# A decoder trunk on one core: softplus behind the evacuation of k, v transposed into the shared score tile, entry weights scaled by ScalarE, the rest scaled in pieces

## The chip, the cores and the metric

The kernel runs on one core of one Trainium2 chip. The metric is the device time of one execution in microseconds. Each of the kernel's versions is timed in several runs, and the median counts.

## The reference

The program is a two-layer decoder trunk over 512 tokens of width 1024: a Mamba-2 layer, then a stick-breaking attention layer, each followed by a gated convolutional feed-forward block and a gated embedding. The change touches the attention and its way in. There, k and v come from one normalised projection, q from another with its own norm gain, and the attention of each of 16 heads is

```
z = einsum("bthd,bshd->bhts", q[:, q0:q1], k[:, :q1]) * scale
log_beta = log_sigmoid(z)
log_keep = where(causal, log_sigmoid(-z), 0.0)
log_rest = cumsum(log_keep, axis=3, reverse=True) - log_keep
w = where(causal, exp(log_beta + log_rest), 0.0)
out = einsum("bhts,bshd->bthd", w, v[:, :q1])
```

## The kernel before

All activations lie transposed: 128 features on the partitions, 512 tokens along the free axis. Every large product is done in three matmuls per 128x128 weight block, high part times low part, low times high, and high times high (L214 to L216), so that one product with 8 blocks is 24 matmuls of 128x512. Weights come from memory in units of 8 blocks, which one DMA loads (`raw`, L82, three buffers). Units of the q, k and v matrices are first multiplied by the norm's gain on GpSimd (L94, one instruction for a run of blocks). Then ScalarE rounds the unit into its high part (`whi`, L103) and VectorE takes the low part as a difference (`wlo`, L104). Units are made two ahead of their use.

The attention goes over 8 pairs of heads, p = 0 to 7. In steady state TensorE's order for one pair is written out by hand:

- the scores of pair p into five PSUM tiles (L754 to L775): one tile of two banks, of which only half of each bank is used (score part n = 0), and four of one bank (parts 1 to 4);
- `att_c(p-1, 0)`, weights times v for the first head of the pair before (L853), then the k product of pair p+1, then `att_c(p-1, 1)`;
- the q product of pair p+1, in whose middle v of pair p is transposed (`v_split`, L733) into an accumulator bank `pv`;
- `att_b(p)`, the suffix sums (L829), which add products of softplus(z) with a triangle of -1 onto the scores, in the order n = 1, 0, 2, 3, 4;
- the v product of pair p+1.

The products and `att_c` and `pv` share two accumulator banks. A product can start when the bank that was used two turns ago has been evacuated.

Between scores and suffix sums stands softplus, in `att_a`. ScalarE takes Abs and Exp of the five parts (L790, L791), loads another function table, and takes Ln (L794). For each part VectorE then adds max(z, 0) (`e`, L797) and rounds the high part (`sh`, L801), and GpSimd takes the low part (`sl`, L802). After the suffix sums ScalarE takes Exp (`w`, L832) and rounds (`wh`), and VectorE takes the low part (`wl`, L835). The other names: `t` is the evacuation of k or q out of the bank (L721) and `v` that of v (L726), `hi` and `lo` are the two parts of k, q or the output (L195, L196), `tp` and `e<-pav` evacuate `att_c` (L858, L859), `ot` is the low part of the output, and `vv` are the two parts of the transposed v (L738 on ScalarE, L739 on VectorE).

Only TensorE's order is by hand. On the other engines a scheduler sets the order when the program is built, from priorities, and each engine then works its queue strictly in that order. `tc.high_priority` moves instructions up, `tc.issue_after(x)` keeps them behind an instruction x.

On the way into the attention the last product of layer 0 (8 output tiles) feeds the residual, the squares for the norm (L230), their sum on GpSimd (`acc_sq`, L233) and on TensorE (`nsum`, L240), the reciprocal root on GpSimd (`ms`), eight small diagonal blocks on VectorE (`dg`), and their spread over the partitions (`nspr`, L275). Meanwhile q and k of pair 0 are multiplied into two further banks, `qa` and `ka`, then k of pair 1.

Of the kernel before, what the change touches and what calls it, by code (L numbers as in the profile page):

```python
# [67 lines left out]
class Weights:  # L68
# [3 lines left out]
    def __init__(self, nc, pool, src, ahead=2):  # L72
        self.nc, self.pool, self.src, self.ahead = nc, pool, src, ahead
        self.units, self.made, self.pos, self.gains = {}, 0, 0, {}

    def make(self, u, between=None):
        nc = self.nc
        raw = self.pool.tile([P, 8, P], F32, tag="raw", name="raw", bufs=3)
        cuts = 2 if u < 1 else 1
        parts = [slice(c * 8 // cuts, (c + 1) * 8 // cuts) for c in range(cuts)]  # L80
        for c, part in enumerate(parts):
            nc.sync.dma_start(  # L82
                out=raw[:, part].rearrange("p k m -> p (k m)"),
                in_=self.src[u][:, c * KD * P // cuts:(c + 1) * KD * P // cuts],
            )
            if between:
                between()
        i = 0
        while i < 8 and PLAN[8 * u][0] in self.gains:
            name, k, _ = PLAN[8 * u + i]  # L90
            n = 1
            while i + n < 8 and PLAN[8 * u + i + n][:2] == (name, k + n):
                n += 1
            nc.gpsimd.tensor_tensor(  # L94
                out=raw[:, i:i + n], in0=raw[:, i:i + n],
                in1=self.gains[name][:, k:k + n].unsqueeze(2).to_broadcast([P, n, P]), op=ALU.mult
            )
# [21 lines left out]
def tile_yoco(ctx: ExitStack, tc: tile.TileContext, xT, pT, prm, cst, csb, wdt, wts, out, dbg=None):  # L119
# [589 lines left out]
    ntri, nones, mask = cr[:, 0:128], cr[:, 128:256], cr[:, 256:512]  # L709
    identr = const.tile([P, P], F32R, name="identr")  # L710
    A.copy(out=identr, in_=ident)
    qs, ks, vs = {}, {}, {}

    def proj(name, m, hooks=None, bank=acc_bank):
        acc = bank()
# [2 lines left out]

    def qk_split(dst, p, acc, scale):
        t = S("t", 2)  # L720
        V.scalar_tensor_tensor(out=t, in0=acc, scalar=scale, in1=n_kv.r, op0=ALU.mult, op1=ALU.mult)  # L721
        dst[p] = split(t)

    def v_evac(p, acc):
        t = S("t", 2, name="v")
        V.tensor_tensor(out=t, in0=acc, in1=n_kv.r, op=ALU.mult)  # L726
        vs[p] = t

    def v_split(p):
        t = vs[p]  # L730
        pv = acc_bank("pv")
        for c in range(NCH):
            PE.transpose(out=pv[:, c * P:(c + 1) * P], in_=t[:, c * P:(c + 1) * P], identity=ident)  # L733
        pv4 = pv.rearrange("p (c i d) -> p c i d", c=NCH, i=2)
        vs[p] = []
        for i in range(2):
            vv = H(F32R, shape=(P, NCH, 2, 64), name="vv")
            A.copy(out=vv[:, :, 0], in_=pv4[:, :, i])  # L738
            V.tensor_tensor(out=vv[:, :, 1], in0=pv4[:, :, i], in1=vv[:, :, 0].bitcast(F32), op=ALU.subtract)  # L739
            vs[p].append(vv)  # L740
# [4 lines left out]

    def scores(p):

        two = two_banks("z")
        zs = [two[:, :, 0:256]] + [aux_bank("z") for _ in range(4)]
        ones_by = {}  # L750
        for n, parts in enumerate(PARTS):
            if n == 0:
                for i in range(2):
                    PE.matmul(two[:, i, 0:P], lhsT=identr, rhs=mask[:, 0:P], start=True, stop=False, skip_group_check=True)  # L754
                    ones_by[n, i] = two[:, i]
            elif n < 3:
                z = zs[n]
                PE.matmul(
                    z.rearrange("p (a b) -> p a b", b=P)[:, 0:2], lhsT=identr,
                    rhs=mask.rearrange("p (a b) -> p a b", b=P), start=True, stop=False, skip_group_check=True,  # L760
                )
            else:
                PE.matmul(zs[n][:, 0:P], lhsT=identr, rhs=mask[:, 0:P], start=True, stop=False, skip_group_check=True)
        todo = []
        for i in range(2):
            at = 0
            for n in TURNS[i]:
                own = [(b, c0 if n else 0) for h, b, c0 in PARTS[n] if h == i]
# [14 lines left out]

    def att_a(p):

        es, sp = {}, {}
        zs = scores(p)
        for n in (2, 0, 1, 3, 4):
            e = es[n] = S("d", 6, name="e") if n < 3 else S("c", 3, name="e")
            A.activation(out=like(n, e), in_=zs[n], func=AF.Abs)  # L790
            last = A.activation(out=e, in_=e, func=AF.Exp, scale=-1.0)  # L791
        with tc.issue_after(last.ins):
            for n in (2, 0, 1, 3, 4):
                ln = A.activation(out=es[n], in_=es[n], func=AF.Ln, bias=1.0)  # L794
        for n in (2, 0, 1, 3, 4):
            e = es[n]
            V.scalar_tensor_tensor(  # L797
                out=like(n, e), in0=zs[n], scalar=0.0, in1=like(n, e), op0=ALU.max, op1=ALU.add
            )
            hi, lo = H(F32R, name="sh"), H(F32R, name="sl")  # L800
            V.tensor_copy(out=hi, in_=e)  # L801
            G.tensor_tensor(out=lo, in0=e, in1=hi.bitcast(F32), op=ALU.subtract)  # L802
            sp[n] = (hi, lo)
        return zs, sp, ln

    def att_b(p, zs, sp, ln):

# [35 lines left out]
    def att_c(p, i, ws, bank=acc_bank):  # L843

        if i == 0:
            ots[p] = S("e", 3)
        ot = ots[p]
        po = bank("pav")
        mm = []
        for b, t_, f0 in ((0, ws[3 + i], 0), (1, ws[1 + i], 128), (2, ws[0], i * 256), (3, ws[1 + i], 0)):  # L850
            mm += [(po[:, b * P:], vs[p][i][:, b], s_[:, f0:f0 + T - b * P]) for s_ in t_]
        for n, (o_, l_, r_) in enumerate(mm):
            PE.matmul(  # L853
                o_, lhsT=l_.rearrange("p a d -> p (a d)"), rhs=r_, start=n == 0, stop=n == len(mm) - 1,
            )
        tp = S("th", 1, name="tp")
        with tc.high_priority(offset=300):
            A.copy(out=tp[0:64], in_=po[64:128])  # L858
            V.tensor_tensor(out=ot[LO[i]], in0=po[0:64], in1=tp[0:64], op=ALU.add)  # L859
        if i:  # L860
            if dbg:
                dbg("o", p, ot)
            o_t.append(split(ot, lo=S("ot", 8, F32R)))

    def qk(name, dst, p, scale, hooks=None):
        acc = proj(name, p, hooks)
        with tc.high_priority(offset=200):
            qk_split(dst, p, acc, scale)

    def v_proj(p):  # L870
        acc = proj("v", p)
        with tc.high_priority(offset=200):
            v_evac(p, acc)

    qa, ka = aux_bank("qa"), aux_bank("ka")
    product(qa, "q", 0, range(7), xg, stop=False)
    product(ka, "k", 0, range(7), xg, stop=False, hooks={5: n_kv.sums})
    product(qa, "q", 0, [7], xg, start=False)
    product(ka, "k", 0, [7], xg, start=False)
    qk("k", ks, 1, 1.0, hooks={3: n_kv.spread})  # L880
    with tc.high_priority(offset=400):
        qk_split(qs, 0, qa, 0.125)
        qk_split(ks, 0, ka, 1.0)
    ws = None
    for p in range(8):
        zz = att_a(p)
        if p:
            att_c(p - 1, 0, ws)
        if 0 < p < 7:
            qk("k", ks, p + 1, 1.0)  # L890
        elif p == 0:
# [115 lines left out]
```

## Time and profile before

| | |
|---|---|
| median of 3 runs | 1605.1 us (1603.92 to 1607.39) |
| the profiled execution | 1602.3 us, its span 1600.4 us |
| TensorE matmul busy | 1516.9 us (95%) |
| VectorE busy | 1023.1 us (64%) |
| ScalarE busy | 756.8 us (47%) |
| GpSimd busy | 345.1 us (22%) |
| mean granted TensorE clock | 0.971 |

The span runs from the first to the last instruction. Times in rows are microseconds from its start. Busy shares are averages over the whole program. The attention takes the stretch from about 840 to 1150 us, and there the mean granted clock of 50 us windows lies between 0.90 and 0.97.

### The profile page before, as it was taken

To read this page: it belongs to the slowest core of one execution; us is meant where nothing else is said; L and a number is where in the kernel's file an instruction comes from. 1 tells how busy PE (TensorE), PEld (TensorE's weight loads), DVE (VectorE), ACT (ScalarE), POOL (GpSimd) and SP (SyncE) were. 2 spreads that over 40 slices of the span, in tenths; PEclk is the share of its full clock that TensorE was granted. 3 is DMA by queue.
4 is the path that set the end of the run, shared out by engine and by line. 5 is a ranking of instruction groups with operands and counts; after the bars stand their busy time and mean duration, and the time that the engine had idled before them with its cause. 6 is when DMAs were issued, how large, how long until landed. Compare 5 with 4: busy or idle time off the path is not lost.

```text
span 1600.4 us, 18433 instructions
## 1 busy us (share of the span) xinstructions
PE 1516.9 (95%) x7082; PEld 1243.4 (78%) x7082; DVE 1023.1 (64%) x1334; ACT 756.8 (47%) x1152; POOL 345.1 (22%) x243
## 2 busy tenths in 40 slices
PE   7889999999999999999997999887999999999996
PEld 5677777788888888888886777776788888888885
DVE  6887888765567766622475876675567766652444
ACT  4365565644344443422444677766444444342343
POOL 3012424431110110101143533331211011010112
PEclk9999999999999999999998999999999999999998
DMA  5233332423333332333331111111233333333321
GB/s 175 78 112 121 97 126 86 125 80 92 94 104 93 93 105 93 111 100 93 93 91 53 53 53 53 40 41 45 72 97 96 95 101 95 96 108 93 94 90 53
DMA packets 44055, 143.67 MB, mean 90 GB/s; under 512 B 4896, under 2 KB 5152, under 8 KB 43968
## 3 DMA queue, kind: packets, MB, share of 16 engines
q1 hardware_dynamic: 43968, 142.51, 28.9%
q8 instruction: 55, 0.90, 0.2%
q14 instruction: 32, 0.26, 0.1%
HBM read 140.32 MB, written 2.16 MB: 89 GB/s over the span
## 4 chain that ended last, share of the span: by engine, by line
PE 75%; DVE 10%; ACT 8%; issue 3%; POOL 3%; DMA 1%; POOLq 0%; SPq 0%; ACTq 0%; DVEq 0%
PE acc L214 23%; PE acc L216 22%; PE acc L215 22%; PE z L829 3%; DVE wlo L104 2%; DVE c L328 2%; ACT d L494 1%; ACT whi L103 1%; DVE sh L801 1%; POOL y L522 1%; DVE e L797 1%; ACT e L790 1%; PE z L775 1%; ACT e L791 1%; DVE t L683 1%
## 5 line engine op out<-in xcount | busy, mean ns | idle before, releaser
L214 PE MATMUL acc<-hi,wlo 128*128 128x512 f32 x1776 | 714.6, 402 | 32.9 <-DVE t L721 19.8
L215 PE MATMUL acc<-lo,whi 128*128 128x512 f32 x1808 | 711.0, 393 | 0.0
L216 PE MATMUL acc<-hi,whi 128*128 128x512 f32 x1776 | 700.8, 395 | 0.0
L104 DVE TENSOR_TENSOR wlo<-raw,whi 128x1024 fp32r<-128x1024 f32 (+1 forms) x240 | 308.0, 1283 | 200.2 <-ACT whi L103 197.5
L214 PEld LDWEIGHTS acc<-hi,wlo 128*128 128x128 f32 x1776 | 339.6, 191 | 107.6 <-DVE t L721 20.7
L103 ACT CAST whi<-raw 128x1024 fp32r<-128x1024 f32 (+1 forms) x241 | 252.1, 1046 | 340.7 <-PE acc L216 285.2
L215 PEld LDWEIGHTS acc<-lo,whi 128*128 128x128 f32 x1808 | 344.5, 191 | 72.5 <-issue 3.4
L216 PEld LDWEIGHTS acc<-hi,whi 128*128 128x128 f32 x1776 | 338.9, 191 | 72.8
L328 DVE SCALAR_TENSOR_TENSOR c<-t,pm,c 128x511 f32<-128x511 f32 (+2 forms) x248 | 188.5, 762 | 5.8 <-ACT c L323 2.0
L233 POOL TENSOR_TENSOR acc_sq<-acc_sq,sq 128x512 f32<-128x512 f32 x60 | 87.1, 1452 | 400.8 <-ACT sq L230 350.6
L634 POOL TENSOR_TENSOR hf<-th,c 128x512 f32<-128x512 f32 x44 | 59.3, 1347 | 427.6 <-DVE c L328 388.2
L323 ACT ACTIVATE c<-t,pm 128x512 f32<-128x512 f32 x112 | 91.1, 814 | 14.1 <-DVE t L321 13.8
L321 DVE TENSOR_TENSOR t<-acc,r 128x512 f32<-128x512 f32 x112 | 76.7, 686 | 30.2 <-PE acc L216 26.7
L802 POOL TENSOR_TENSOR sl<-e,sh 128x512 fp32r<-128x512 f32 x40 | 57.5, 1439 | 86.3 <-DVE sh L801 83.1
L195 ACT CAST hi<-hf 128x512 fp32r<-128x512 f32 x44 | 26.8, 618 | 95.0 <-POOL hf L634 95.0
L94 POOL TENSOR_TENSOR raw<-raw,pm 128x1024 f32<-128x1024 f32 (+3 forms) x27 | 52.5, 1949 | 82.4 <-DMA raw<-in_wts 73.0
L196 DVE TENSOR_TENSOR lo<-hf,hi 128x512 fp32r<-128x512 f32 x44 | 32.3, 738 | 59.3 <-ACT hi L195 59.3
L631 ACT ACTIVATE th<-c 128x512 f32<-128x512 f32 x44 | 27.8, 632 | 80.8 <-DVE c L328 80.8
L494 ACT ACTIVATE d<-d,tok 128x128 f32<-128x128 f32 x128 | 44.7, 392 | 13.3 <-DMA d<-rows 12.8
L498 POOL TENSOR_TENSOR d<-d,cb 128x512 f32<-128x512 f32 x16 | 25.3, 1586 | 117.7 <-ACT btok L445 69.1
L632 DVE SCALAR_TENSOR_TENSOR th<-th,c 128x512 f32<-128x512 f32 x44 | 30.4, 691 | 30.6 <-ACT th L631 30.6
L230 ACT ACTIVATE sq<-x_k 128x512 f32<-128x512 f32 (+1 forms) x50 | 30.5, 615 | 34.5 <-DVE x_k L282 20.8
(193 smaller groups left out, 1522.6 us busy)
## 6 DMA issues: line engine op xcount, KB each, us to landing
raw<-in_wts SPq DMA_DIRECT2D x239, 512.0 KB, 3.6
d<-rows SPq DMA_DIRECT2D x32, 256.0 KB, 3.7
x_k<-in_xT SPq DMA_DIRECT2D x16, 256.0 KB, 4.9
out<-xo SPq DMA_DIRECT2D x8, 256.0 KB, 2.8
p_k<-in_pT SPq DMA_DIRECT2D x4, 256.0 KB, 3.0
raw<-in_wts SPq DMA_DIRECT2D x2, 256.0 KB, 4.1
pm<-in_prm SPq DMA_DIRECT2D x1, 312.0 KB, 6.4
cbt<-in_csb SPq DMA_DIRECT2D x1, 256.0 KB, 4.7
```

The source lines that it names most:

```text
L103: nc.scalar.copy(out=hi[:, part], in_=raw[:, part])
L104: e.tensor_tensor(out=lo[:, part], in0=raw[:, part], in1=hi[:, part].bitcast(F32), op=ALU.subtract)
L214: PE.matmul(acc, lhsT=wl, rhs=xh, start=start and n == 0, stop=False)
L215: PE.matmul(acc, lhsT=wh, rhs=xl, start=False, stop=False)
L216: PE.matmul(acc, lhsT=wh, rhs=xh, start=False, stop=stop and n == len(ks) - 1)
L233: G.tensor_tensor(out=self.acc, in0=self.acc, in1=t, op=ALU.add)
L321: V.tensor_tensor(out=t, in0=acc, in1=r, op=ALU.mult)
L323: A.activation(out=c, in_=t, func=AF.Identity, scale=w[:, f * taps + taps - 1:f * taps + taps], bias=b[:, f:f + 1])
L328: V.scalar_tensor_tensor(out=c[:, s:], in0=t[:, :T - s], scalar=w[:, i:i + 1], in1=c[:, s:], op0=ALU.mult, op1=ALU.add)
L494: A.activation(out=d[:, cs], in_=d[:, cs], func=AF.Relu, scale=-1.0, bias=acs[:, c * 32 + h:c * 32 + h + 1])
L634: G.tensor_tensor(out=hf, in0=th, in1=c1, op=ALU.mult)
L802: G.tensor_tensor(out=lo, in0=e, in1=hi.bitcast(F32), op=ALU.subtract)
```

## The change

Four edits are made together.

- Softplus is cut out of `att_a` into a function of its own that is called after `att_c(p-1, 1)`. Its VectorE instructions are kept behind the evacuation of the k product (of the v product for p = 0, of `att_c(6, 0)` for p = 7).
- v is transposed into the unused halves of the two-bank score tile (part 0). The bank `pv` is gone. The ScalarE and VectorE instructions that read the transposed v (`vv`) get a high priority.
- The weight units up to the second one from the start of k of pair 1 (four units) are scaled by ScalarE, in eight instructions of 128x128 each. The later units (twenty) stay on GpSimd, in pieces of 128x256, four for a unit.
- q and k of pair 0 are evacuated and split inside the product for k of pair 1, ahead of that product's own evacuation.

```diff
+        self.act_until = PLAN.index(("k", 0, 1)) // 8 + 2
...
+            if u < self.act_until:
+                for j in range(i, i + n):
+                    nc.scalar.activation(
+                        out=raw[:, j], in_=raw[:, j], func=AF.Identity, scale=self.gains[name][:, k + j - i:k + j - i + 1]
+                    )
+            else:
+                for j in range(i, i + n, 2):
+                    e = min(j + 2, i + n)
+                    nc.gpsimd.tensor_tensor(
+                        out=raw[:, j:e], in0=raw[:, j:e],
+                        in1=self.gains[name][:, k + j - i:k + e - i].unsqueeze(2).to_broadcast([P, e - j, P]),
+                        op=ALU.mult,
+                    )
...
     def v_split(p):
         t = vs[p]
-        pv = acc_bank("pv")
+        pv = twos.pop(p)[:, :, 256:512]
         for c in range(NCH):
-            PE.transpose(out=pv[:, c * P:(c + 1) * P], in_=t[:, c * P:(c + 1) * P], identity=ident)
+            PE.matmul(
+                pv[:, c // 2, c % 2 * P:(c % 2 + 1) * P], lhsT=t[:, c * P:(c + 1) * P], rhs=ident,
+                is_transpose=True, start=False, stop=False, skip_group_check=True,
+            )
...
+        with tc.high_priority(offset=300):
+            for i in range(2):
+                vv = H(F32R, shape=(P, NCH, 2, 64), name="vv")
+                v5 = vv.rearrange("p (a c) h d -> p a c h d", a=2)
+                src = pv4[:, :, :, i]
+                A.copy(out=v5[:, :, :, 0], in_=src)
+                V.tensor_tensor(out=v5[:, :, :, 1], in0=src, in1=v5[:, :, :, 0].bitcast(F32), op=ALU.subtract)
+                vs[p].append(vv)
...
-        two = two_banks("z")
+        two = twos[p] = two_banks("z")
...
+        return zs, es, ln
+
+    def softplus(zs, es):
+        sp = {}
         for n in (2, 0, 1, 3, 4):
...
-    qk("k", ks, 1, 1.0, hooks={3: n_kv.spread})
-    with tc.high_priority(offset=400):
-        qk_split(qs, 0, qa, 0.125)
-        qk_split(ks, 0, ka, 1.0)
+    def first():
+        n_kv.spread()
+        with tc.high_priority(offset=400):
+            qk_split(qs, 0, qa, 0.125)
+            qk_split(ks, 0, ka, 1.0)
+
+    qk("k", ks, 1, 1.0, hooks={3: first})
...
-        zz = att_a(p)
+        zs, es, ln = att_a(p)
         if p:
-            att_c(p - 1, 0, ws)
+            evac = att_c(p - 1, 0, ws)
         if 0 < p < 7:
-            qk("k", ks, p + 1, 1.0)
+            evac = qk("k", ks, p + 1, 1.0)
         elif p == 0:
-            v_proj(0)
+            evac = v_proj(0)
         if p:
             att_c(p - 1, 1, ws)
+        with tc.issue_after(evac.ins):
+            sp = softplus(zs, es)
```

The order on VectorE in pair 3, from the evacuation of `att_c(2, 0)` on. Before:

```order
L859 TENSOR_TENSOR e<-pav,tp 64x512
L797 SCALAR_TENSOR_TENSOR e<-z,e 128x512 x2
L801 CAST sh<-e 128x512
L797 SCALAR_TENSOR_TENSOR e<-z,e 128x512
L801 CAST sh<-e 128x512
L797 SCALAR_TENSOR_TENSOR e<-z,e 128x512
L721 SCALAR_TENSOR_TENSOR t<-acc,r 128x512
```

Now:

```order
L880 TENSOR_TENSOR e<-pav,tp 64x512
L731 SCALAR_TENSOR_TENSOR t<-acc,r 128x512
L818 SCALAR_TENSOR_TENSOR e<-z,e 128x512 x2
L206 TENSOR_TENSOR lo<-t,hi 128x512
L880 TENSOR_TENSOR e<-pav,tp 64x512
L818 SCALAR_TENSOR_TENSOR e<-z,e 128x512
L822 CAST sh<-e 128x512
L206 TENSOR_TENSOR ot<-e,hi 128x512
```

The evacuation `t` of k moved ahead of all of softplus. The low part of k, the evacuation of `att_c(2, 1)` and `ot` moved in between, ahead of the first or second `sh`.

The same queue up to `vv` in the same pair (the second `t` is the evacuation of q). Before:

```order
L801 CAST sh<-e 128x512
L859 TENSOR_TENSOR e<-pav,tp 64x512
L801 CAST sh<-e 128x512
L104 TENSOR_TENSOR wlo<-raw,whi 128x1024
L196 TENSOR_TENSOR lo<-t,hi 128x512
L196 TENSOR_TENSOR ot<-e,hi 128x512
L739 TENSOR_TENSOR vv<-pv,vv 128x4x64 x2
L721 SCALAR_TENSOR_TENSOR t<-acc,r 128x512
L104 TENSOR_TENSOR wlo<-raw,whi 128x1024
```

Now:

```order
L822 CAST sh<-e 128x512
L818 SCALAR_TENSOR_TENSOR e<-z,e 128x512
L822 CAST sh<-e 128x512
L818 SCALAR_TENSOR_TENSOR e<-z,e 128x512
L822 CAST sh<-e 128x512
L114 TENSOR_TENSOR wlo<-raw,whi 128x1024
L731 SCALAR_TENSOR_TENSOR t<-acc,r 128x512
L822 CAST sh<-e 128x512
L114 TENSOR_TENSOR wlo<-raw,whi 128x1024
L756 TENSOR_TENSOR vv<-z,vv 128x4x64 x2
```

The evacuation of q and the second `wlo` moved from behind `vv` to ahead of it.

The order on ScalarE in the same pair, from the last Ln on. Before:

```order
L794 ACTIVATE e<-e 128x512 x5
L103 CAST whi<-raw 128x1024
L858 COPY tp<-pav 64x512
L195 CAST hi<-t 128x512
L195 CAST hi<-e 128x512
L738 CAST vv<-pv 128x4x64 x2
L103 CAST whi<-raw 128x1024
L195 CAST hi<-t 128x512
L832 ACT_TABLE_LOAD
L832 ACTIVATE w<-z 128x512
```

Now:

```order
L811 ACTIVATE e<-e 128x512 x5
L113 CAST whi<-raw 128x1024
L205 CAST hi<-t 128x512
L879 COPY tp<-pav 64x512
L205 CAST hi<-e 128x512
L113 CAST whi<-raw 128x1024
L853 ACT_TABLE_LOAD
L853 ACTIVATE w<-z 128x512
L755 CAST vv<-z 128x4x64 x2
```

The two `vv` copies moved behind the first `w`, the Exp of part 1, which waits for the suffix sums of part 1 on TensorE.

On TensorE the order is the same in both. One wait on it is new in each pair: the first suffix sum of part 0 (L850 now, L829 before) waits for the second `vv` on VectorE, since both use the two-bank tile. On GpSimd each pair has its five `sl`, then the scaling of three units, in both; in three instructions before, in twelve now. On the way in, the sum of the last squares now stands behind the four pieces of one unit, and the reciprocal root behind those of a second.

## Rows read from the trace of the kernel before

**Rows 1.** TensorE's waits between 840 and 1240 us: total, times, longest.

```profile
PE acc L214 <- DVE t L721: 19.8, 6, 3.3
PE acc L214 <- DVE vv L739: 5.4, 1, 5.4
PE z L763 <- DVE t L721: 4.6, 2, 3.6
PE nsum L240 <- POOL acc_sq L233: 3.8, 1, 3.8
```

**Rows 2.** Stretches of pair 3: length, busy time by engine, granted clock, DMA.

```profile
973.55:979.54 5.99, 5.99 (x17) 4.72 (x17) 5.93 (x7) 1.21 (x2) 4.71 (x4) 0.50 0.00 0
979.54:993.18 13.64, 13.64 (x75) 11.84 (x73) 9.55 (x12) 9.29 (x15) 4.44 (x3) 1.00 0.26 78
```

**Rows 3.** The chain of waits: start, length; scores of pair 1, of pair 7.

```profile
894.47 2.11 PE z L775 x18
...
1093.28 1.07 PE z L775 x6
```

**Rows 4.** TensorE in pair 3 by time: start, length, line, tiles, shapes.

```profile
959.17 0.33 PE L754 MATMUL z<-cr,identr 128*128 128x128 f32 x2
...
968.63 0.39 PE L216 MATMUL acc<-hi,whi 128*128 128x512 f32 x1
...
982.41 0.39 PE L829 MATMUL z<-sh,cr 128*128 128x512 f32 x1
...
983.32 0.40 PE L829 MATMUL z<-sh,cr 128*128 128x256 f32 x2
...
987.66 0.45 PE L214 MATMUL acc<-hi,wlo 128*128 128x512 f32 x1
...
993.18 0.33 PE L754 MATMUL z<-cr,identr 128*128 128x128 f32 x2
```

**Rows 5.** VectorE in pair 3 by time.

```profile
968.95 1.29 DVE L797 SCALAR_TENSOR_TENSOR e<-z,e 128x512 f32<-128x512 f32 x2 [2.31 <-ACT e L794]
970.15 0.42 DVE L801 CAST sh<-e 128x512 fp32r<-128x512 f32 x1
...
971.09 1.21 DVE L801 CAST sh<-e 128x512 fp32r<-128x512 f32 x1
...
977.34 1.21 DVE L104 TENSOR_TENSOR wlo<-raw,whi 128x1024 fp32r<-128x1024 f32 x1
978.48 1.76 DVE L196 TENSOR_TENSOR lo<-t,hi 128x512 fp32r<-128x512 f32 x1
...
981.61 0.42 DVE L739 TENSOR_TENSOR vv<-pv,vv 128x256 fp32r<-128x256 f32 x1 [0.44 <-ACT vv L738]
```

**Rows 6.** GpSimd in pair 3 by time.

```profile
970.74 1.27 POOL L802 TENSOR_TENSOR sl<-e,sh 128x512 fp32r<-128x512 f32 x1 [3.30 <-DVE sh L801]
...
977.57 2.12 POOL L802 TENSOR_TENSOR sl<-e,sh 128x512 fp32r<-128x512 f32 x1 [0.43 <-DVE sh L801]
```

**Rows 7.** ScalarE in pair 3 by time.

```profile
968.28 2.71 ACT L794 ACTIVATE e<-e 128x512 f32<-128x512 f32 x5
970.90 1.03 ACT L103 CAST whi<-raw 128x1024 fp32r<-128x1024 f32 x1
...
981.21 0.37 ACT L738 CAST vv<-pv 128x256 fp32r<-128x256 f32 x1 [0.99 <-DVE vv L739]
...
985.53 0.60 ACT L832 ACTIVATE w<-z 128x512 f32<-128x512 f32 x1
```

**Rows 8.** All scalings of L94: ns shortest/median/longest, first and last start, shapes.

```profile
L94 POOL TENSOR_TENSOR raw<-raw,pm x27: 843/1899/2894, 814.1 to 1033.3; 128x1024 f32<-128x1024 f32 x22, 128x128 f32<-128x128 f32 x3, 128x896 f32<-128x896 f32 x1, 128x768 f32<-128x768 f32 x1
```

**Rows 9.** ScalarE's 128x128 activations elsewhere: busy us, mean ns.

```profile
L494 ACT ACTIVATE d<-d,tok 128x128 f32<-128x128 f32 x128 | 44.7, 392 | 13.3 <-DMA d<-rows 12.8
```

**Rows 10.** VectorE in pair 7: the first two `e`.

```profile
1102.73 1.29 DVE L797 SCALAR_TENSOR_TENSOR e<-z,e 128x512 f32<-128x512 f32 x2 [1.26 <-ACT e L794]
```

**Rows 11.** TensorE in pair 7: the first suffix sum.

```profile
1118.61 0.39 PE L829 MATMUL z<-sh,cr 128*128 128x512 f32 x1
```

More of the change, by code (lines that the diff above doesn't have):

```diff
@@ L93, in make @@
                 n += 1
[L94 to L97, printed above, removed]
+            if u < self.act_until:
[11 more added lines that the diff above has]
+                    )
             i += n
@@ L711, in tile_yoco @@
     A.copy(out=identr, in_=ident)
-    qs, ks, vs = {}, {}, {}
+    qs, ks, vs, twos = {}, {}, {}, {}
     def proj(name, m, hooks=None, bank=acc_bank):
@@ L720, in qk_split @@
         t = S("t", 2)
-        V.scalar_tensor_tensor(out=t, in0=acc, scalar=scale, in1=n_kv.r, op0=ALU.mult, op1=ALU.mult)
+        evac = V.scalar_tensor_tensor(out=t, in0=acc, scalar=scale, in1=n_kv.r, op0=ALU.mult, op1=ALU.mult)
         dst[p] = split(t)
+        return evac
     def v_evac(p, acc):
         t = S("t", 2, name="v")
-        V.tensor_tensor(out=t, in0=acc, in1=n_kv.r, op=ALU.mult)
         vs[p] = t
+        return V.tensor_tensor(out=t, in0=acc, in1=n_kv.r, op=ALU.mult)
     def v_split(p):
         t = vs[p]
-        pv = acc_bank("pv")
+        pv = twos.pop(p)[:, :, 256:512]
         for c in range(NCH):
-            PE.transpose(out=pv[:, c * P:(c + 1) * P], in_=t[:, c * P:(c + 1) * P], identity=ident)
-        pv4 = pv.rearrange("p (c i d) -> p c i d", c=NCH, i=2)
-        vs[p] = []
[L736 to L740, printed above, removed]
+            PE.matmul(
+                pv[:, c // 2, c % 2 * P:(c % 2 + 1) * P], lhsT=t[:, c * P:(c + 1) * P], rhs=ident,
+                is_transpose=True, start=False, stop=False, skip_group_check=True,
+            )
+        pv4 = pv.rearrange("p a (c i d) -> p a c i d", c=2, i=2)
+        vs[p] = []
+        with tc.high_priority(offset=300):
[6 more added lines that the diff above has]
+                vs[p].append(vv)
     PARTS = [[(0, 2, 0), (1, 2, 256)], [(0, 3, 0), (0, 1, 128)], [(1, 3, 0), (1, 1, 128)], [(0, 0, 0)], [(1, 0, 0)]]
@@ L784, in att_a @@
     def att_a(p):
-        es, sp = {}, {}
+        es = {}
         zs = scores(p)
@@ L803, in att_a @@
             sp[n] = (hi, lo)
-        return zs, sp, ln
+        return sp
     def att_b(p, zs, sp, ln):
@@ L858, in att_c @@
             A.copy(out=tp[0:64], in_=po[64:128])
-            V.tensor_tensor(out=ot[LO[i]], in0=po[0:64], in1=tp[0:64], op=ALU.add)
+            evac = V.tensor_tensor(out=ot[LO[i]], in0=po[0:64], in1=tp[0:64], op=ALU.add)
         if i:
@@ L863, in att_c @@
             o_t.append(split(ot, lo=S("ot", 8, F32R)))
+        return evac
     def qk(name, dst, p, scale, hooks=None):
@@ L867, in qk @@
         with tc.high_priority(offset=200):
-            qk_split(dst, p, acc, scale)
+            return qk_split(dst, p, acc, scale)
     def v_proj(p):
@@ L872, in v_proj @@
         with tc.high_priority(offset=200):
-            v_evac(p, acc)
+            return v_evac(p, acc)
     qa, ka = aux_bank("qa"), aux_bank("ka")
@@ L902, in tile_yoco @@
                 product(accs[m], "o", m, range(6), o_t, stop=False)
-        ws = att_b(p, *zz)
+        ws = att_b(p, zs, sp, ln)
         if p < 7:
```

## Prediction

> **What bounds the kernel now.** I read the busy shares first: TensorE is the bound outside the attention, so only stretches where it waits or runs at half clock can move the time. Then TensorE's own waits in the attention [rows 1]: 19.8 us in six equal waits, one in each of pairs 1 to 6, where the q product waits for the evacuation `t` of the k bank, which stands in VectorE's queue between softplus instructions; 5.4 us in pair 7; 4.6 and 3.8 us on the way in. Then the clock by stretches of one pair [rows 2]: the wait is followed by 5.99 us at a granted clock of 0.50 (1.2 GHz), and from 979.54 on the clock is 1.00 (2.4 GHz) again. So the price of such a wait is the wait and about half of that slow stretch: 3.31 + 3.0 = 6.3 us in pair 3. That pair lasts 993.18 - 959.17 = 34.0 us [rows 4], so its work at full clock is 27.7 us. The mean of pairs 1 to 6 is (1093.28 - 894.47) / 6 = 33.1 us [rows 3], so a mean pair loses 5.4 us: 3.3 waiting and 2.1 by the clock.
>
> Next VectorE and GpSimd side by side. A `sh` takes 0.42 us at 970.15 and 1.21 us at 971.09 [rows 5]; in the second case GpSimd's `sl` runs from 970.74 to 972.01 [rows 6], and `sh` ends 0.29 us after it. The other way round, the `sl` at 977.57 takes 2.12 us instead of 1.27, since `wlo` holds VectorE from 977.34 for 1.21 us; then `lo` at 978.48 takes 1.76 us, until after that `sl` has ended at 979.69. So `sh`, `lo`, `ot` and `wlo` exclude GpSimd's instructions, for a whole instruction. The Trainium skill says so too (SBUF — State Buffer, "Who interferes with whom"): the shared port pair is an exclusive lock that the first to issue keeps to its end. By a rule of no exclusion the walk below would come out 2.7 us shorter for each pair; that case is the second rival.
>
> **Pairs 1 to 6, the main term.** The wait for `t` goes: k ends at 968.63 + 0.39 = 969.02 [rows 4], `t` follows at once, and att_c and q run on without a stop. TensorE would then be at the suffix sums at 982.41 - 6.3 = 976.1, and at those of part 0 at 983.32 - 6.3 = 977.0 if nothing else were late. What is late next is softplus and, behind it, `vv`. I walk VectorE's new queue on the clock of pair 3, whose first 10 us are the same in both kernels; an instruction out of PSUM counts 0.6 (two `e` in 1.29), a free `sh` 0.35, a free `lo` or `ot` 0.6, `wlo` 1.15, since followers start a little before the end shown.
>
> - `t` and two `e`: 969.06 + 3 x 0.6 = 970.9.
> - Now `lo` of k needs its `hi`. That is on ScalarE behind Ln (to 970.99) and `whi` (to 971.9) [rows 7], takes 0.6, and so ends at 972.5. VectorE stands still for 1.6 us; behind `lo` is all the rest of softplus.
> - `lo`, the evacuation of att_c, one `e`, `sh`, `ot`: 972.5 + 0.6 + 0.6 + 0.6 + 0.35 + 0.6 = 975.3.
> - From here `sh` and `sl` take turns, 1.7 us for a turn (1.28 for `sl`, 0.28 for the rest of `sh`, 0.15 until the next `sl`): the first `sl` ends at 976.5, the second `sh` at 976.7, the third at 978.5, its `sl`, of part 1, at 979.9. TensorE's second suffix sum of part 1 waits for that one.
> - An `e` and the fourth `sh` to 980.2, `wlo` to 981.3, `t` of q to 981.9; the fifth `sh` waits for the `sl` that `wlo` held up and ends at 982.7; the second `wlo` ends at 983.9, the first `vv` at 984.2. ScalarE's second `vv` copy (0.37) and VectorE's second `vv` (0.42) follow: 985.1. Before, `vv` was through at 982.03, with two fewer instructions ahead of it and no still stand.
>
> Only then may the suffix sums of part 0 start: 985.1 instead of 977.0. Even with VectorE free they would wait, since the `vv` copies stand behind Exp of part 1 on ScalarE: 0.60 + 0.37 + 0.42 + 0.37 + 0.42 [rows 5, 7] = 2.2 us. The pair waits 8.1 us where it waited 3.3. The clock falls in this as it did in the wait before, and the sums of parts 0 to 4 and the start of the v product run at half clock; I take 2.5 us (between the mean 2.1 and 3.0). A pair loses 10.6 instead of 5.4, so +5.2; six pairs +31. The bounds: with no exclusion at all the same sum of VectorE's queue gives 982.4 for 985.1, +2.5 for a pair, or about 0 if the clock also held; if GpSimd goes first in each contest and its pieces reach into the walk, up to 2 us more, +7.
>
> The Trainium skill (PSUM — Partial Sum Buffer, "PSUM bank collisions raise a hardware error") says that a bank is to be guarded as a whole, not by address. The trace of before shows no wait of this kind, as `pv` had its own bank. With a guard by address the sums of part 0 would start when those of part 1 end, and a pair would lose about 4 us less; the order of the changed kernel has the wait.
>
> **The way in and pair 0.** Before: 3.8 for `nsum` and 4.6 for the scores of pair 0 [rows 1], and after each a slow stretch, 2.8 and 2.3 at the price of rows 2: 13.5 us. After: `nsum` waited because the last evacuations on VectorE stood behind scalings on GpSimd of up to 2.9 us [rows 8]; four units now go to ScalarE, 8 x 0.39 = 3.1 us each [rows 9], beside products of 5.5 us each (24 matmuls, 993.18 - 987.66 [rows 4]), where ScalarE has room. q and k of pair 0 are split during a product, so the 4.6 goes as well. Against that the reciprocal root now stands behind two units' pieces. No row shows a 128x256 piece: it lies between the shortest scaling, 0.84, and a whole unit, 1.90 [rows 8]; by a straight line between these two about 1.0, so 4 us for a unit. `nspr` comes 2 us late if the eight `dg` run free, and 6 us, with a slow stretch behind, if each takes turns with a piece. I take a loss of 3.7, so a gain of 9.8 (bounds 4 and 12). Pair 0 then meets the new order: by the same walk without k and att_c its part 0 starts 21.1 us after its scores start, where TensorE would need 15.2; 5.9 and 2.5 for the clock, less the 0.5 that it lost before: +7.9. Together -1.9 (bounds -9 and +5).
>
> **Pair 7.** The 5.4 goes, since `pv` no longer takes a bank. But the transposes now wait for the second `e`, 1102.73 + 1.29 = 1104.0 [rows 10]. Then transposes 0.4, 36 matmuls 8.2 and 2.5 for the clock: 1115.1, against 1118.61 [rows 11], so -3.5 (bounds -6 and 0).
>
> **The pieces in the rest.** Twenty units in four pieces cost GpSimd 4.0 for 1.9 us each, about 42 us more. They lie behind the `sl` and end before the next softplus; `wl` are delayed by up to 1 us each, with some 8 us until they are needed. So 0; in the softplus they would cost up to 4 us a pair.
>
> **The sum.** 31 - 1.9 - 3.5 = +25.8. On the profiled execution, 1602.3 us, that is 1628. The three timed runs lie 1.6 to 5.1 above it, their median 1605.1 by 2.8, so a median of about 1630.
>
> **Rivals.** About 3.2 us (0.2%) is what a measurement here can tell from no change.
>
> 1. The walk holds: slower, 1618 to 1645. Chance 0.66.
> 2. VectorE gets through GpSimd better than rows 5 and 6 say, the clock falls still: 6 x 2.5 - 6 = +9, 1614. For it: my walk strings up eight contests by a few rows. Against: each contest in pair 3 went to a whole instruction. Chance 0.13.
> 3. Not slower: VectorE takes the port first each time, the waits before part 1 and part 0 shrink to 2.8 and 2.7, and the clock stays at 1.00 in them. A pair loses 5.5, as before, pair 0 some 3, and the gain on the way in and in pair 7 is left: 1595 to 1600. It decides from the point where part 0 starts before 982.4 with the clock kept, or before 980 with the clock fallen. Against it: with nothing in its way VectorE is at `vv` no earlier. Chance 0.12.
> 4. The pieces fall into softplus, since their DMAs start when `wlo` is done, and that moves: up to 4 us more a pair, 1645 to 1655. Chance 0.09.
>
> The first, the second and the fourth are slower but for a part of the second. Slower 0.83, same 0.05, faster 0.12. The range 1604 to 1648 leaves out most of the third and the upper half of the fourth.
>
> **What would show it.** In the profile after: no wait of the q product for `t`; instead in each pair two waits at the suffix sums, one for `sl` of some 3 us and one for `vv` of some 4; half clock during the suffix sums, not during q; pairs of 38 us; `vv` on ScalarE right after the first `w`. Scores of pair 0 start near 858. The prediction is wrong if part 0 starts less than 23 us after the pair's scores, if the clock reads 1.00 in the suffix sums, or if GpSimd's pieces leave VectorE's `sh` at 0.42.

## The result and the profile after

The changed kernel takes 1624.16 us (median of 4 runs, 1622.04 to 1625.0), the kernel before beside it 1604.51 us. The ratio is 1.0119, with a 95% interval of 1.01 to 1.0138: slower. The profiled execution of the changed kernel has a span of 1622.5 us, 22.1 more than before, and a mean granted clock of 0.963.

First what TensorE waits for, in the stretch of [rows 1] (total, times, longest).

```profile
PE z L850 <- DVE vv L756: 25.3, 7, 4.2
PE z L850 <- DVE sh L822: 15.4, 6, 2.6
PE z L744 <- DVE e L818: 6.0, 1, 6.0
PE z L850 <- POOL sl L823: 5.8, 7, 0.9
...
PE nspr L285 <- DVE dg L277: 0.2, 1, 0.2
```

All four kinds of [rows 1] are gone. L850 is the suffix sums, L744 the transposes. In each of pairs 1 to 6 the sums of part 1 now wait 2.6 us for a `sh` and up to 0.9 for its `sl`, and those of part 0 wait 3.5 us or so for `vv`: 7.0 us where 3.3 went to `t`.

The chain of waits gives the length of the pairs (start of the scores of pairs 1 and 7, as in [rows 3]).

```profile
889.17 2.11 PE z L792 x18
...
1119.03 1.07 PE z L792 x6
```

Pair 1 starts 5.3 us earlier than before, and a pair lasts (1119.03 - 889.17) / 6 = 38.3 us where it lasted 33.1. From there to the end it is 503.5 us, before 507.1. So -5.3 + 31.1 - 3.7 = +22.1 us, the whole difference of the spans. The first of these terms holds a difference that lies ahead of the edits. The `nsum` of the norm before stands 24 us ahead of the first scaling [rows 8], and the profiled execution of the changed kernel reaches it at 791.44, that of the kernel before at 789.68. Runs with the same way in differ there as much (788.16 in scalar_vv_first, 790.55 in by_hand). Counted from that `nsum`, pair 1 starts 7.1 us earlier.

Pair 3 by engine, in the order of [rows 4 to 7]. TensorE, with what a wait ended on in brackets:

```profile
984.30 0.80 PE L850 MATMUL z<-sh,cr 128*128 128x512 f32 x1 [2.50 <-DVE sh L822]
985.71 0.80 PE L850 MATMUL z<-sl,cr 128*128 128x512 f32 x1 [0.62 <-POOL sl L823]
...
990.87 0.80 PE L850 MATMUL z<-sh,cr 128*128 128x256 f32 x2 [3.51 <-DVE vv L756]
```

The pair's first matmul is at 964.72, so part 0 starts 26.15 us after it. A matmul of 128x512 takes 0.80 us here and took 0.39 at the same place before [rows 4].

VectorE in the same pair:

```profile
978.04 0.69 DVE L206 TENSOR_TENSOR lo<-t,hi 128x512 fp32r<-128x512 f32 x1 [1.55 <-ACT hi L205]
...
981.02 1.50 DVE L822 CAST sh<-e 128x512 fp32r<-128x512 f32 x1
...
983.05 1.19 DVE L822 CAST sh<-e 128x512 fp32r<-128x512 f32 x1
...
985.86 1.21 DVE L114 TENSOR_TENSOR wlo<-raw,whi 128x1024 fp32r<-128x1024 f32 x1
986.99 0.68 DVE L731 SCALAR_TENSOR_TENSOR t<-acc,r 128x512 f32<-128x512 f32 x1
987.59 0.89 DVE L822 CAST sh<-e 128x512 fp32r<-128x512 f32 x1
988.40 1.21 DVE L114 TENSOR_TENSOR wlo<-raw,whi 128x1024 fp32r<-128x1024 f32 x1
989.54 0.41 DVE L756 TENSOR_TENSOR vv<-z,vv 128x256 fp32r<-128x256 f32 x1
990.39 0.42 DVE L756 TENSOR_TENSOR vv<-z,vv 128x256 fp32r<-128x256 f32 x1 [0.44 <-ACT vv L755]
```

Here is the cause in one view. `lo` of k holds the whole of softplus for 1.55 us, since its `hi` is late. Behind softplus stand `wlo`, `t`, `sh`, `wlo`, 3.7 us of work, and only then `vv`, on which TensorE is waiting.

GpSimd: one piece-wise scaling, and two `sl`.

```profile
971.14 2.33 POOL L103 TENSOR_TENSOR raw<-raw,pm 128x256 f32<-128x256 f32 x4 [11.64 <-DMA raw<-in_wts]
...
984.39 1.27 POOL L823 TENSOR_TENSOR sl<-e,sh 128x512 fp32r<-128x512 f32 x1 [0.43 <-DVE sh L822]
986.08 2.12 POOL L823 TENSOR_TENSOR sl<-e,sh 128x512 fp32r<-128x512 f32 x1 [0.43 <-DVE sh L822]
```

The `sl` at 984.39 is that of part 1, for which the sums at 985.71 wait. The four pieces at 971.14 take 2.33 us together; VectorE runs one instruction of 0.68 us beside them. All 80 pieces (ns shortest/median/longest, as in [rows 8]):

```profile
L103 POOL TENSOR_TENSOR raw<-raw,pm x80: 606/614/1594, 837.6 to 1049.7; 128x256 f32<-128x256 f32 x80
```

The `sl` beside the `wlo` of 985.86 takes 2.12 us, as in [rows 6].

ScalarE, and the clock by stretches (columns as in [rows 2]):

```profile
987.40 0.60 ACT L853 ACTIVATE w<-z 128x512 f32<-128x512 f32 x1 [3.17 <-PE z L850]
987.89 0.37 ACT L755 CAST vv<-z 128x256 fp32r<-128x256 f32 x1
989.98 0.37 ACT L755 CAST vv<-z 128x256 fp32r<-128x256 f32 x1 [1.73 <-DVE vv L756]
```

```profile
984.30:994.50 10.20, 6.08 (x21) 4.99 (x22) 8.08 (x11) 3.48 (x7) 8.80 (x8) 0.50 0.34 104
994.50:1003.28 8.78, 8.78 (x49) 7.56 (x48) 3.88 (x5) 4.18 (x7) 2.92 (x4) 1.00 0.01 2
```

After the first wait the clock is at 1.2 GHz until 994.5. TensorE works 6.08 us in that stretch, so in pair 3 the clock takes about 3.0 us on top of the waits. For a mean pair this gives 27.7 + 7.0 + 3.0 = 37.7 of the 38.3 us. The rest is clock as well: TensorE is busy for 31.4 us in a mean pair, and for 28.0 in by_hand below, where the clock reads 1.00.

### The profile page after: what moved, and what is told of

Same layout as the page of the kernel before. It is cut to its first block, busy times and chain, and to the rows that moved or that the text cites. A ratio compares the mean times of both kernels' runs of the same rounds, so it can differ in the third digit from the quotient of the medians.

```text
span 1622.5 us, 18512 instructions
## 1 busy us (share of the span) xinstructions
PE 1522.0 (94%) x7082; PEld 1246.6 (77%) x7082; DVE 1006.2 (62%) x1334; ACT 766.5 (47%) x1184; POOL 360.4 (22%) x296
## 4 chain that ended last, share of the span: by engine, by line
PE 74%; DVE 11%; ACT 7%; issue 4%; POOL 3%; DMA 1%; POOLq 0%; SPq 0%; ACTq 0%; DVEq 0%
PE acc L224 22%; PE acc L225 22%; PE acc L226 22%; PE z L850 3%; DVE wlo L114 2%; DVE c L338 2%; DVE sh L822 1%; ACT whi L113 1%; ACT d L504 1%; DVE e L818 1%; PE z L792 1%; POOL y L532 1%; ACT e L811 1%; PE pav L874 1%; ACT th L357 1%
## 5 line engine op out<-in xcount | busy, mean ns | idle before, releaser
L114 DVE TENSOR_TENSOR wlo<-raw,whi 128x1024 fp32r<-128x1024 f32 (+1 forms) x240 | 298.9, 1246 | 196.9 <-ACT whi L113 194.7
L850 PE MATMUL z<-sh,cr 128*128 128x256 f32 (+3 forms) x144 | 56.0, 409 | 40.6 <-DVE vv L756 25.3
L823 POOL TENSOR_TENSOR sl<-e,sh 128x512 fp32r<-128x512 f32 x40 | 64.4, 1612 | 105.3 <-DVE sh L822 105.3
L103 POOL TENSOR_TENSOR raw<-raw,pm 128x256 f32<-128x256 f32 x80 | 60.9, 793 | 67.6 <-DMA raw<-in_wts 65.7
L850 PEld LDWEIGHTS z<-sh,cr 128*128 128x128 f32 x144 | 37.6, 268 | 47.2 <-DVE vv L756 27.2
L850 PE MATMUL z<-sl,cr 128*128 128x256 f32 (+3 forms) x144 | 52.3, 406 | 5.8 <-POOL sl L823 5.8
L856 DVE TENSOR_TENSOR wl<-w,wh 128x512 fp32r<-128x512 f32 x40 | 32.3, 807 | 32.1 <-ACT wh L855 30.9
```

The source lines that it names most:

```text
L103: nc.gpsimd.tensor_tensor(out=raw[:, j:e], in0=raw[:, j:e], in1=self.gains[name][:, k + j - i:k + e - i].unsqueeze(2).to_broadcast([P, e - ...
L850: PE.matmul(o_, lhsT=l_, rhs=r_, start=False, stop=k == len(mm) - 1, skip_group_check=True)
```

## The experiments

Theory: each of the two large edits is harmless to pairs 1 to 6 by itself. Softplus behind k pushes `vv` back on VectorE; the shared tile makes TensorE wait for `vv` in the same pair; only both together cost. Rivals: one of the two edits costs by itself; the pieces on GpSimd cost; the guard of the shared tile or the port costs whatever the order is. Times are medians; ratios are to the kernel before, on the same chip (1602.7 to 1604.2 us).

| label | us | ratio, 95% interval | mean pair, us |
|---|---|---|---|
| entry_alone | 1587.95 | 0.9903, 0.9888 to 0.9918 | 33.1 |
| softplus_alone | 1603.37 | 1.0003, 0.9991 to 1.0014 | 33.3 |
| shared_tile_alone | 1608.59 | 1.0028, 1.0017 to 1.0038 | 33.0 |
| whole_units | 1623.69 | 1.0125, 1.0109 to 1.014 | 38.4 |
| own_bank | 1589.69 | 0.9906, 0.989 to 0.9922 | 33.6 |
| softplus_in_place | 1593.16 | 0.9931, 0.9908 to 0.9953 | 33.4 |
| scalar_vv_first | 1621.65 | 1.0112, 1.0094 to 1.0131 | 38.2 |
| vv_ahead | 1598.99 | 0.9971, 0.9958 to 0.9984 | 35.1 |
| by_hand | 1559.43 | 0.9718, 0.9703 to 0.9732 | 28.5 |
| k_low_early | 1587.86 | 0.9896, 0.9872 to 0.9919 | 33.5 |
| by_hand_whole | 1554.74 | 0.9707, 0.9678 to 0.9736 | 28.5 |

**One edit alone, on the kernel before: entry_alone.**

```diff
+        self.act_until = PLAN.index(("k", 0, 1)) // 8 + 2
...
+            if u < self.act_until:
+                for j in range(i, i + n):
+                    nc.scalar.activation(
...
-    qk("k", ks, 1, 1.0, hooks={3: n_kv.spread})
+    qk("k", ks, 1, 1.0, hooks={3: first})
```

> The kernel before with the way-in edits alone: four weight units scaled by ScalarE, q and k of pair 0 split inside the k product of pair 1. Softplus, v's own bank and whole-unit scaling on GpSimd stay as before. Theory (what costs is the place of softplus and vv in the queues): the way in is a gain by itself, and the 5.3 us seen at the scores of pair 1 is what was left of it after pair 0 met the new order. The scores of pair 0 start near 855, pairs 1 to 6 stay at 33.1 us, and the time is 13 us under before: about 1592 us (1588 to 1596). Rival (the way-in edits are worth only the 5.3 us that the changed kernel shows): 1599 us.

Measured: 15 us faster, just under the range that I expected. The scores of pair 1 start at 879.27, 15.2 us earlier than in [rows 3], or 13.9 earlier counted from the `nsum` before (here at 788.37). Pair 0 lasts 27.2 us from its first score product to that of pair 1, and 33.8 in the changed kernel. So the new order costs pair 0 6.6 us; the rest of the way from -15.2 to -5.3 is 3.1 us that lie ahead of that `nsum` and 0.2 for `nspr`.

**softplus_alone.**

```diff
-        zz = att_a(p)
+        zs, es, ln = att_a(p)
...
+        with tc.issue_after(evac.ins):
+            sp = softplus(zs, es)
```

> The kernel before with one edit: softplus behind the evacuation of k. v keeps its own bank, the way in and the scaling are as before. Theory (two waits, one for each of two edits): TensorE waits only for the sl of part 1, 2.6 to 3.4 us in each pair with half clock behind it, in place of the 3.3 us for t; part 0 does not wait for vv. A pair comes to 33 to 34.5 us and the time to 1606 us (1601 to 1614). Rival (the move of softplus alone costs what the change costs, and the shared tile is innocent): pairs of 38 us, 1630 us or more.

Measured: no change. TensorE and VectorE in pair 3:

```profile
980.54 0.49 PE L841 MATMUL z<-sh,cr 128*128 128x512 f32 x1 [1.40 <-DVE sh L813]
981.96 0.50 PE L841 MATMUL z<-sl,cr 128*128 128x512 f32 x1 [0.92 <-POOL sl L814]
...
982.75 0.40 PE L841 MATMUL z<-sh,cr 128*128 128x256 f32 x2
```

```profile
984.67 1.22 DVE L111 TENSOR_TENSOR wlo<-raw,whi 128x1024 fp32r<-128x1024 f32 x1
...
986.66 0.42 DVE L747 TENSOR_TENSOR vv<-pv,vv 128x256 fp32r<-128x256 f32 x1 [0.44 <-ACT vv L746]
```

`vv` is as late as in the changed kernel, but part 0 starts at 982.75, 4.3 us before `vv` is done: with a bank of its own nobody waits for it. What I expected of the clock holds in half of the pairs only. In pair 3, as in 1 and 6, it reads 1.00 through these waits and behind them (4.1 us in four pieces, with one of 0.93 at the transposes and one of 0.82 in part 4). In pairs 2, 4 and 5 it falls to 0.50 behind waits of the same size (1.0, 1.4 and 0.9 us). Pairs 2 and 3 whole, columns as in [rows 2]:

```profile
927.00:961.74 34.74, 31.44 (x160) 26.30 (x160) 24.72 (x30) 22.58 (x38) 14.40 (x8) 0.90 0.15 46
961.74:994.50 32.76, 28.70 (x160) 23.55 (x160) 22.90 (x28) 22.25 (x38) 14.57 (x8) 1.00 0.16 49
```

**shared_tile_alone.**

```diff
-        pv = acc_bank("pv")
+        pv = twos.pop(p)[:, :, 256:512]
...
+        with tc.high_priority(offset=300):
             for i in range(2):
```

> The kernel before with one edit: v transposed into the spare halves of the two-bank tile, vv with high priority. Softplus is in its old place, so vv stands ahead of the second wlo on VectorE and ahead of the first w on ScalarE, as before. Theory: the new wait of part 0 for vv costs nothing, since vv is through by 982 and part 0 starts at 983.3; pairs stay at 33.1 us, the 5.4 us wait of pair 7 goes, and the time is 1601 us (1598 to 1604). Rival (sharing the tile by itself costs the 4 us a pair seen at vv): 1628 us.

Measured: 5 us slower, where I expected a few us faster. Pairs 1 to 6 last as long as before, pair 7 gains 3.0, but pair 0 loses: the scores of pair 1 start at 902.73, 8.3 us later than in [rows 3]. VectorE and TensorE in pair 0:

```profile
882.72 1.21 DVE L111 TENSOR_TENSOR wlo<-raw,whi 128x1024 fp32r<-128x1024 f32 x1
883.86 1.48 DVE L819 CAST sh<-e 128x512 fp32r<-128x512 f32 x1
885.26 0.68 DVE L728 SCALAR_TENSOR_TENSOR t<-acc,r 128x512 f32<-128x512 f32 x1
885.86 1.97 DVE L111 TENSOR_TENSOR wlo<-raw,whi 128x1024 fp32r<-128x1024 f32 x1
887.75 0.41 DVE L753 TENSOR_TENSOR vv<-z,vv 128x256 fp32r<-128x256 f32 x1
```

```profile
889.08 0.80 PE L847 MATMUL z<-sh,cr 128*128 128x256 f32 x2 [5.54 <-DVE vv L753]
```

It is the theory's mechanism: in pair 0 `vv` stands behind both `wlo` with softplus in its old place too. The forecast had looked only at pairs 1 to 6. There too `vv` comes with no time to spare. In pairs 3 and 6 the clock stays at 1.00 behind the 3.3 us wait for `t`, TensorE is at part 0 sooner, and it waits there for `vv`, in pair 3 so:

```profile
990.71 0.50 PE L847 MATMUL z<-sh,cr 128*128 128x256 f32 x2 [1.45 <-DVE vv L753]
```

These two pairs are no shorter than the other four (32.9 us).

**One edit undone: whole_units.**

```diff
-                for j in range(i, i + n, 2):
-                    e = min(j + 2, i + n)
-                    nc.gpsimd.tensor_tensor(
-                        out=raw[:, j:e], in0=raw[:, j:e],
+                nc.gpsimd.tensor_tensor(
+                    out=raw[:, i:i + n], in0=raw[:, i:i + n],
```

> The changed kernel with one edit undone: GpSimd scales each unit in one instruction and not in four pieces. Theory (the order of VectorE and ScalarE costs, the pieces do not): 1624 us (1620 to 1629), pairs of 38.3 us, waits for vv of about 4 us and for sl of about 3 us as in the changed kernel. Rival (the pieces take the port from VectorE in softplus): pairs lose 1 us or more of the 5.2 us, 1600 to 1618 us.

Measured: as the changed kernel, to 0.1%. The pieces are no cause.

**own_bank.**

```diff
-        pv = twos.pop(p)[:, :, 256:512]
+        pv = acc_bank("pv")
```

> The changed kernel with one edit undone: v is transposed into a bank of its own again; softplus behind k, the way in and the pieces stay. Theory (the move of softplus and the shared tile each cost nothing in pairs 1 to 6, the two together cost 5.2 us a pair, since only then TensorE waits for vv at a place in VectorE's queue that softplus has pushed back): pairs of 33.3 us, no wait of part 0 for vv, and the gain of the way in is left: 1588 us (1584 to 1594). Rival (it is softplus with the new way in, or with the pieces, that costs): pairs over 35 us and 1605 us or more.

Measured: 34 us less than the changed kernel, by this edit alone, which also takes back the high priority of `vv`. TensorE's waits from 880 to 1090 us:

```profile
PE z L844 <- DVE sh L816: 8.4, 6, 1.4
PE pv L744 <- DVE e L874: 7.7, 7, 1.9
PE z L844 <- POOL sl L817: 7.1, 8, 0.9
```

No wait for `vv`, and that for `sh` is 1.4 where it was 2.6, since about 1.0 us has already gone at the transposes, which wait for a bank.

**softplus_in_place.**

```diff
-        with tc.issue_after(evac.ins):
-            sp = softplus(zs, es)
...
         zs, es, ln = att_a(p)
+        sp = softplus(zs, es)
```

> The changed kernel with the other edit undone: softplus in its old place, v in the spare halves, the way in and the pieces as changed. Theory: pairs of 33 us with the 3.3 us wait for t back; pair 0 loses some 5 to 8 us, as where the shared tile was alone, pair 7 gains 3: 1593 us (1586 to 1598). Rival (sharing the tile costs by itself as soon as the way in is short): 1610 us or more.

Measured: 30 us less than the changed kernel, by undoing the other edit. Together with own_bank this shows that the cost belongs to neither edit but to the pair of them. The sum of the edits alone, by their ratios, is -15.6 + 0.5 + 4.5 = -10.6 us; together they make +19.1. The 30 us between are 6 x 5.

**The order altered: scalar_vv_first.** The first `w` behind the `vv` copies, on ScalarE alone.

```diff
-            with tc.issue_after(ln.ins):
+            with tc.issue_after(vlast[0].ins if n == 1 else ln.ins):
                 A.activation(out=like(n, w), in_=z, func=AF.Exp)
```

> The changed kernel with one order altered, on ScalarE alone: the first w of a pair is held behind the two vv copies. VectorE's order stays. Theory (VectorE's queue decides, vv there stands behind wlo, t, sh and wlo): vv is through at the same time, some 26 us after the pair's scores, since the second copy on ScalarE waits for the first vv of VectorE anyway; pairs of 38 to 38.5 us, 1624 us (1619 to 1628). Rival (the place of vv behind w on ScalarE is a good part of the cost): pairs under 37 us, 1612 us or less.

Measured: as the changed kernel. ScalarE in pair 3:

```profile
978.68 0.37 ACT L757 CAST vv<-z 128x256 fp32r<-128x256 f32 x1
985.71 0.37 ACT L757 CAST vv<-z 128x256 fp32r<-128x256 f32 x1 [6.66 <-DVE vv L758]
```

The first copy is made at once, and the second then waits 6.66 us for VectorE's first `vv`. ScalarE's order is not the cause.

**vv_ahead.** Both `wlo` and the evacuation of q behind `vv` on VectorE, the first `w` behind it on ScalarE.

```diff
+        held, wt.held = wt.held, None
+        with tc.issue_after(vlast[1].ins):
+            for f in held:
+                f()
...
+            with tc.issue_after(vlast[1].ins), tc.high_priority(offset=200):
+                qk_split(qs, p + 1, acc, 0.125)
```

> The changed kernel, with vv put first: on VectorE both wlo of the pair and the evacuation of q are held behind vv, on ScalarE the first w is. All edits stay. Theory (the queue behind which vv stands is the cost): vv is through some 2 to 3 us earlier, at 22.5 to 24 us after the pair's scores in place of 26.1; the wait for sl of part 1 stays; pairs of 35 to 36.5 us, 1606 us (1600 to 1614). Rival (the guard of the shared tile, or the port, costs whatever the order): no pair under 37.5 us, 1618 us or more.

Measured: 24 us less than the changed kernel by the two ratios, 1 us below the range that I expected; a pair is 3.2 us shorter. The waits from 790 to 1260 us:

```profile
PE z L858 <- DVE sh L830: 15.4, 6, 2.6
...
PE z L858 <- POOL sl L831: 5.2, 7, 0.9
...
PE z L858 <- DVE vv L760: 1.9, 7, 0.9
```

The wait for `vv` fell from 25.3 to 1.9 us; those for `sh` and `sl` stayed. The guard of the shared tile is there in both, so it costs only by the order.

**by_hand.** All four edits, with the rest of VectorE's order turned round too.

```diff
+    ORDER = [(2, "e"), (0, "e"), (2, "h"), (1, "e"), (0, "h"), (3, "e"), (1, "h"), (4, "e"), (3, "h"), (4, "h")]
...
+                with tc.issue_after(last.ins):
+                    if op == "e":
+                        last = V.scalar_tensor_tensor(
...
+        last = rest(last)
+        held, wt.held = wt.held, None
+        with tc.issue_after(last.ins):
+            for f in held:
+                f()
```

> All four edits, with VectorE's order in each pair held as TensorE needs it: evacuation of k, then softplus (e and sh in the order 2, 0, 1, 3, then 4), vv ahead of the last sh, and only then the low part of k, the evacuation and split of the second att_c, the evacuation of q and the wlo; vv ahead of the first w on ScalarE. Theory: neither the wait for t nor those for sl and vv are left beyond 1 us, the clock holds, pairs come to 28 to 30 us (full-clock work was 27.7), and the time to 1562 us (1552 to 1575). Rival (GpSimd's sl and the port set the pace of softplus whatever the order): part 1 still waits about 3 us and falls to half clock, pairs of 33 us, 1588 us.

Measured: 45 us faster than the kernel before and, by the two ratios, 64 faster than the changed kernel. TensorE's waits from 883 to 1060 us, and one pair on TensorE and VectorE:

```profile
PE z L867 <- DVE vv L765: 3.1, 6, 0.5
```

```profile
956.52 0.39 PE L867 MATMUL z<-sh,cr 128*128 128x512 f32 x1
...
958.18 0.51 PE L867 MATMUL z<-sh,cr 128*128 128x256 f32 x2 [0.52 <-DVE vv L765]
```

```profile
955.73 1.20 DVE L840 CAST sh<-e 128x512 fp32r<-128x512 f32 x1
...
957.70 0.42 DVE L765 TENSOR_TENSOR vv<-z,vv 128x256 fp32r<-128x256 f32 x1 [0.44 <-ACT vv L763]
```

One wait of 0.5 us is left in a pair. The `sh` beside `sl` still take 1.2 us, so the port is as contended as ever; it fits, since nothing else stands between them. Of the moves beyond those of vv_ahead, only that of the low part of k is shown by itself, in the next run.

**k_low_early.** by_hand, with `lo` of k back ahead of the first `sh`.

```diff
+            last = softplus(zs, es, sp, ORDER[:2], evac)
...
+                with tc.issue_after(last.ins):
+                    evac = V.tensor_tensor(out=lo, in0=t, in1=hi.bitcast(F32), op=ALU.subtract)
```

> The order held by hand, with one instruction moved back to where the changed kernel has it: in pairs 1 to 6 the low part lo of k stands behind the first two e of softplus, ahead of the first sh. Theory (VectorE stands still there for about 1.6 us, since lo waits for hi, which is on ScalarE behind Ln and a whi; with lo itself, 2.2 us): the sl of part 1 comes 2 us late, part 1 waits about 1.5 us, and the clock falls behind it: pairs of 30 to 32.5 us in place of 28.5, 1577 us (1568 to 1584). Rival (the stall falls into slack): 1560 us.

Measured: 28 us more than by_hand, where I expected 18. The direction is the theory's, the size was off. TensorE and the clock in pair 2:

```profile
933.21 0.51 PE L867 MATMUL z<-sh,cr 128*128 128x512 f32 x1 [0.90 <-DVE sh L840]
934.62 0.50 PE L867 MATMUL z<-sl,cr 128*128 128x512 f32 x1 [0.91 <-POOL sl L841]
...
936.10 0.79 PE L867 MATMUL z<-sh,cr 128*128 128x256 f32 x2 [0.52 <-DVE vv L765]
```

```profile
936.10:942.10 6.00, 6.00 (x23) 5.61 (x24) 5.56 (x8) 5.35 (x9) 1.45 (x2) 0.50 0.27 82
```

Three waits come to 2.3 us, 1.8 more than in by_hand. Behind them the clock is at 0.50 for 6.0 us and a little longer, and TensorE is busy for 31.6 us in this pair where by_hand has 28.0: 3.6 more. So this pair loses 5.4 us; the mean of the six is 4.9 (33.45 for 28.52). I had taken 1.5 us of waiting and less of the clock.

**by_hand_whole.** by_hand, with the scaling in whole units.

```diff
-                for j in range(i, i + n, 2):
+                nc.gpsimd.tensor_tensor(
```

> The order held by hand, with GpSimd's scaling in whole units again in place of pieces. Theory (the scalings lie behind the wl and end before the next sl, whole or cut): 1559 us (1556 to 1563). Rival (with so little slack in softplus the shorter pieces matter): 1565 us or more.

Measured: 1554.74 us, 1 us below the range that I expected; its interval and that of by_hand overlap, so whole units are not shown to be better, and pieces have no use here. Both versions beat both kernels.

## Why the prediction was right

It said 1630 us, and 1624 were measured. Step by step:

- **The wait of q for `t` goes, two waits at the suffix sums take its place.** Right. Part 0 starts 26.15 us after the pair's first matmul; the walk gave 985.1 - 959.17 = 25.9. The steps between agree too: `lo` of k starts 13.3 us after that matmul, as in the walk, and the `sl` of part 1 ends 20.9 us after it (walk: 20.7). A pair lasts 38.3 us, as forecast; the waits are 7.0 us and not 8.1, the clock 3.0 to 3.4 and not 2.5. Those two errors nearly cancel. Of the wait at part 1, forecast as one for `sl`, most ends on the `sh` ahead of that `sl` (2.6 us and up to 0.9). That the clock falls in every pair came true, but it was no rule: in shared_tile_alone a wait of 3.3 us left the clock at 1.00 in two pairs of six.
- **`lo` of k waits 1.6 us for `hi`.** Measured 1.55. That it matters where this order leaves no slack is shown by k_low_early: the still stand and `lo` itself cost 4.9 us a pair there.
- **`sh`, `wlo` and `sl` exclude each other.** Right: `sh` takes 1.50 and 1.19 us beside an `sl`, `sl` 2.12 behind a `wlo`. So the second and the third rival fell, and the fourth by the line on the pieces below.
- **Part 0 waits for the second `vv`.** Right, 3.51 us in pair 3. The Trainium skill's rule (PSUM — Partial Sum Buffer, "PSUM bank collisions raise a hardware error"), a guard by bank and not by address, agrees with the trace here, where the program waits so; what would come of it without the guard no run shows. The same section names ScalarE against VectorE, two readers, too; in the trace ScalarE's second copy waits 1.73 us for VectorE's first `vv`.
- **"Even with VectorE free they would wait, since the `vv` copies stand behind Exp of part 1 on ScalarE".** This did not enter the sum, and it gave ScalarE too much weight: with the copies ahead of that Exp the time stays (scalar_vv_first). With VectorE's order turned as well, `vv` costs 0.3 us a pair (vv_ahead). VectorE's order alone was not tried.
- **The way in.** The term was mis-sized: I took a gain of 9.8 us, bounds 4 and 12, and entry_alone gains 13.9 counted from the `nsum` before, 15 by the medians. The loss that I subtracted for `nspr`, 3.7 us, is 0.2 in the changed kernel, and the waits with their slow stretches go altogether. Pair 0 was put at +7.9; it costs 33.8 - 27.2 = 6.6. Both errors go the same way: -1.9 forecast, -7.1 measured from the same `nsum`. The scores of pair 0 start at 854.7, forecast near 858.
- **Pair 7.** -3.5 forecast, -3.7 measured; the transposes wait 6.0 us for the second `e`, as said.
- **The pieces.** 0 forecast, 0 measured. The size behind it was wrong: a piece was put at 1.0 us by a straight line through [rows 8], but the median of the 80 is 0.61, the mean 0.79.

The sum was +25.8, the span grew by 22.1 and the median by 19.7. Against the span the way in and pair 0 were 5.2 us too high, and 1.8 us of the growth lie ahead of the edits.

## What to carry to other kernels

Two edits of which neither lengthens a pair by itself can cost 5 us a pair together, when one delays an instruction and the other makes somebody wait for it; so before a buffer is shared, look up in the queue of its last reader what stands ahead. A wait moved off one place in a tight pair comes back at the next late instruction, and what decides is the order on the engine that feeds TensorE: the same edits with VectorE's queue in the order in which TensorE needs the results gave 45 us where the scheduler's order lost 20. Work that nobody awaits soon (`wlo`, the low part of k, `ot`) goes behind work that TensorE awaits, even where it is ready first.

## What the runs showed of the hardware that I had not expected

- The same waits do not always bring half clock. In softplus_alone waits of 1.0, 1.4 and 0.9 us left the clock at 1.00 in pairs 1, 3 and 6 and were followed by 0.50 in pairs 2, 4 and 5. In shared_tile_alone the wait of 3.3 us left it at 1.00 in pairs 3 and 6, while in the kernel before it fell behind that wait in all six pairs. In k_low_early three waits of 2.3 us were followed by 6 us at 0.50. What tells these apart stays open. Pairs 2 and 3 of softplus_alone last 34.74 and 32.76 us.
- A 128x256 scaling on GpSimd takes 0.61 us at the median, though no scaling of [rows 8], the 128x128 among them, took less than 0.84.
- ScalarE's 32 scalings of 128x128 take 387 ns each by the profile but keep it busy for only 9.7 us, 0.30 each, as each starts before the end of the one ahead. Together eight cost 2.4 us, where the prediction took 3.1.
